# Scores of 64 new queries against 320 keys: from two full-precision matmuls with the queries as 64 weight columns each to four split-precision matmuls with the high and low queries side by side

## The chip, the cores and the metric

The kernel runs on one core of one Trainium2 chip. A core has TensorE (PE, matrix products, with weight loads shown as PEld), VectorE (DVE), ScalarE (ACT), GpSimd (POOL), and SyncE (SP), whose queue issues most DMA transfers. The engines run side by side; each takes its own instructions strictly in order and waits on semaphores for the others. The metric is the time of one execution on the device in microseconds (us), as the median of several executions; lower is better.

## What is computed

One layer of a streaming encoder for two groups that share all weights: the Prompt (256 positions) and the Sample (64 new positions behind 256 cached ones). The two are held together as 320 columns. The layer is a norm, a projection into q, k, v, two gating branches, stick-breaking attention, a spatial gate, a merge, an output projection, and a feed-forward block. The part that matters here is the attention, for each of 8 heads of width 128:

```python
z = einsum('bqhd,bkhd->bhqk', q, k) * 128 ** -0.5
mask = k_pos[None, :] < q_pos[:, None]
log_beta = log_sigmoid(z)
log_stay = where(mask, log_sigmoid(-z), 0.0)
log_rest = cumsum(log_stay, axis=3, reverse=True) - log_stay
w = where(mask, exp(log_beta + log_rest), 0.0)
o = einsum('bhqk,bkhd->bqhd', w, v)
```

For the Sample, q has 64 rows, and k has 320: 64 of its own and 256 from the cache. The mask cuts only inside the 64 own keys. All inputs and outputs are float32.

## The kernel before

Activations lie with the features on the 128 partitions and the 320 positions along the free axis. The large products keep float32 accuracy in a faster type: every operand is split into a high part (rounded to the type `float32r`, by ScalarE) and a low part (the rest, by VectorE), and three matmuls, high x high, high x low, low x high, add up in PSUM (`product`, lines 83 to 85). `weights` loads a half block of 128 x 1024 weights on SP's queue (line 70) and splits it: the copy to `wh` on ScalarE (line 75), the subtraction to `wl` on VectorE (line 76). Raw tiles have three buffers, split ones four, so loads and splits run some half blocks ahead of TensorE. A block of 16 row tiles is two half blocks of 24 matmuls.

`tick()` counts half blocks. `at(n, fn)` asks that `fn` is written into the program after half block n, so the attention's small steps are strewn between the matmuls of the projections. The program text is then turned into one order per engine by a scheduler that uses its own estimates of durations; instructions inside `keep_in_program_order` keep theirs.

The eight heads go in four pairs p. Pair 0 is projected in the opening phase. Each later pair takes twelve half blocks, k, q, v of one head and then of the other; `head_out` evicts each from PSUM, and GpSimd issues the stores of k and v (line 478). For a pair, `att_keys` loads the cached keys behind the new ones in the tile `k`; `att_parts` splits the Prompt's second query block and its keys with `parts`, which takes its tiles from the 32 slots of tag "B"; `att_scores` makes the scores. In `att_scores` the PSUM tiles `za` receive the Prompt's scores (one full float32 matmul for the diagonal block, line 387, and three split ones, line 389, for each head). The PSUM tile `zs` receives the Sample's: one full float32 matmul for each head (line 391), with the head's 64 queries as weights, so that head 0 writes rows 0 to 63 and head 1 rows 64 to 127. Lines 395 to 398 move the scores into two SBUF tiles z, adding a mask of large negative numbers where keys are hidden: `z[0]` gets the 256 past keys of the Sample, `z[1]` its 64 own ones.

What follows is a chain over these tiles: |z| (line 403), exp (404), ln (405) on ScalarE, then on VectorE line 406, backward running sums (413) and a subtraction (416), exp again on ScalarE (417 to 420), then the turning of the weights by DMA and the products with v (`att_out`). `attend` sets the half blocks at which these steps are written. There are eight PSUM banks: three tiles "acc" for the projections, four "aux", one "aux1".

Of the kernel before, what the change touches and what calls it, by code (L numbers as in the profile page):

```python
# [8 lines left out]
F32 = mybir.dt.float32  # L9
F32R = mybir.dt.float32r  # L10
AF = mybir.ActivationFunctionType
ALU = mybir.AluOpType

P = 128
TP = 256
TS = 64
T = TP + TS
# [7 lines left out]
PAST = 256  # L25
# [8 lines left out]
def stream_step(ctx: ExitStack, tc: tile.TileContext, xT, w_in, w_a, w_b, w_out, w_gu, w_down,  # L34
                gains, ws_t, bs, ck_t, cv, y_t, k_t, v_t, sv_t):
    nc = tc.nc
# [11 lines left out]
    def aux():  # L48
        return psum.tile([P, 512], F32, tag="aux", bufs=4, name="aux")
# [5 lines left out]
    state = {"tick": 0}  # L55
    later: dict[int, list] = {}

    def at(tick, fn, *a):
        assert tick > state["tick"], (tick, state["tick"])
        later.setdefault(tick, []).append((fn, a))  # L60
# [26 lines left out]
    def block(src, act):  # L87

        ps = acc()
        nk = len(act)  # L90
        for k0 in range(0, nk, HALF):
            n = min(HALF, nk - k0)
            w = weights(src[:, k0 * P : (k0 + n) * P], n)
            for j in range(n):
                product(ps, w, j, act[k0 + j], k0 + j == 0, k0 + j == nk - 1)
            tick()
        return ps[:, :T]

    def slot(tag):
        return big.tile([P, T], F32R, tag=tag, bufs=32, name=tag)  # L100

    def pair(name):
        return big.tile([P, 2 * T], F32, tag="D", bufs=8, name=name)
# [24 lines left out]
    def t320(tag, bufs=2, dt=F32):  # L128
        return tmp.tile([P, T], dt, tag=tag, bufs=bufs, name=tag)
# [92 lines left out]
    def use_w(b, wh, wl, c, n):  # L222

        for w, parts, last in ((wh, (0, 1), False), (wl, (0,), True)):
            for j in range(n):
                for h in range(2):
                    for i in parts:
                        nc.tensor.matmul(first[b][h][:, :T], w[:, (h * n + j) * P : (h * n + j + 1) * P],  # L228
                                         xs[c + j][i], start=not last and c + j + i == 0,
                                         stop=last and c + j == KD - 1)  # L230
# [61 lines left out]
    attn = {}  # L292
# [23 lines left out]
    Z, KT = 384, T + PAST  # L316
# [5 lines left out]
    mown = apool.tile([P, TS], F32, name="mown")  # L322
# [3 lines left out]
    ROWS = (slice(0, TS), slice(TS, P))  # L326
# [3 lines left out]
    def att_new(p):  # L330
        attn[p] = {"q": apool.tile([P, 2, T], F32, tag="q", bufs=2, name="q"),
                   "k": apool.tile([P, 2, KT], F32, tag="k", bufs=2, name="k"),
                   "v": apool.tile([P, 2, T], F32, tag="v", bufs=2, name="v")}
# [5 lines left out]
    def planes(name, n):  # L339
        return pair(name)[:, 0:n].bitcast(U16).rearrange("p (w n) -> p w n", w=2)  # L340

    def apart(to, src):
        nc.scalar.copy(out=to, in_=src.bitcast(U16).rearrange("p (n w) -> p w n", w=2))
# [18 lines left out]
        tc.keep_in_program_order(nc.sync.dma_start(out=cvt.rearrange("p i h d -> p i (h d)"),  # L362
                                                   in_=cv[:, :, 2 * p * P : (2 * p + 2) * P]))

    def parts(src):

        n = src.free_size()
        hi, lo = (slot("B")[:, 0:n] for _ in range(2))
        view = lambda t: t.rearrange("p (j d) -> p j d", j=src.shape[1]) if len(src.shape) == 3 else t
        nc.scalar.copy(out=view(hi), in_=src)  # L370
        nc.vector.tensor_tensor(out=view(lo), in0=src, in1=view(hi.bitcast(F32)), op=ALU.subtract)
        return hi, lo


# [2 lines left out]
    def att_parts(p):  # L377
        s = attn[p]
        s["qp"] = parts(s["q"][:, :, P:TP])
        s["kp"] = [parts(s["k"][:, j, 0:TP]) for j in range(2)]  # L380

    def att_scores(p):
        s = attn[p]
        q, k, qp = s["q"], s["k"], s["qp"]
        za, zs = (aux(), aux()), aux()
        for j in range(2):
            nc.tensor.matmul(za[j][:, 0:P], q[:, j, 0:P], k[:, j, 0:P], start=True, stop=True)  # L387
            for a, b in THREE:
                nc.tensor.matmul(za[j][:, P:Z], qp[a][:, j * P : (j + 1) * P], s["kp"][j][b], start=a + b == 0, stop=a == 1)  # L389
        for j, r in enumerate(ROWS):  # L390
            nc.tensor.matmul(zs[r, 0 : KT - TP], q[:, j, TP:T], k[:, j, TP:KT], start=True, stop=True)  # L391
        z = s["z"] = pair("z0"), pair("z1")[:, 0 : Z + TS]
        for j in range(2):
            diag = [t[:, 0:Z].rearrange("p (i t) -> p i t", i=3)[:, 0:3:2, :] for t in (z[j], za[j])]
            nc.vector.tensor_tensor(out=diag[0], in0=diag[1], in1=mdiag.unsqueeze(1).broadcast_to([P, 2, P]), op=ALU.add)
            nc.vector.tensor_copy(z[j][:, P : 2 * P], za[j][:, P : 2 * P])
        nc.vector.tensor_tensor(out=z[1][:, Z:], in0=zs[:, 0:TS], in1=mown, op=ALU.add)
        nc.vector.tensor_copy(z[0][:, Z:], zs[:, TS : TS + PAST])

        es = []  # L400
        for zz in z:
            e = pair("e")[:, : zz.shape[1]]
            nc.scalar.activation(out=e, in_=zz, func=AF.Abs)
            nc.scalar.activation(out=e, in_=e, func=AF.Exp, scale=-1.0)
            nc.scalar.activation(out=e, in_=e, func=AF.Ln, bias=1.0)
            nc.vector.scalar_tensor_tensor(out=e, in0=zz, scalar=0.0, in1=e, op0=ALU.max, op1=ALU.add)
            es.append(e)


        for j, lo, hi, begin in ((0, 0, P, 0.0), (0, P, Z, 0.0), (1, 0, P, 0.0), (1, P, Z, 0.0),  # L410
                                 (1, Z, Z + TS, 0.0), (0, Z, Z + PAST, es[1][:, Z : Z + 1])):
            back = es[j][:, lo:hi][:, ::-1]
            nc.vector.tensor_tensor_scan(out=back, data0=ones[:, 0:1].broadcast_to([P, hi - lo]), data1=back,
                                         initial=begin, op0=ALU.mult, op1=ALU.add)
        for zz, e in zip(z, es):
            nc.vector.tensor_tensor(out=zz, in0=zz, in1=e, op=ALU.subtract)
        nc.scalar.activation(out=z[0], in_=z[0], func=AF.Exp)
        nc.scalar.activation(out=z[1][:, 0:Z], in_=z[1][:, 0:Z], func=AF.Exp)
        for r in ROWS:
            nc.scalar.activation(out=wown[r, r], in_=z[1][r, Z:], func=AF.Exp)  # L420

        y = s["wp"] = planes("wp0", 5 * P), planes("wp1", 4 * P)
        apart(y[0], z[0])
        apart(y[1][:, :, 0:Z], z[1][:, 0:Z])
        apart(y[1][:, :, Z:], wown)
# [44 lines left out]
    def head_out(name, ps, h):  # L470
        s = attn[h // 2]
        o = s[name][:, h % 2, 0:T]
        if name == "q":
            nc.vector.scalar_tensor_tensor(out=o, in0=ps, scalar=QSCALE, in1=got["rx"],
                                           op0=ALU.mult, op1=ALU.mult)
        else:
            nc.vector.tensor_tensor(out=o, in0=ps, in1=got["rx"], op=ALU.mult)
            nc.gpsimd.dma_start(out=(k_t if name == "k" else v_t)[h], in_=o)
        if name == "v":
            j = h % 2  # L480
            if j == 0:
                s["vp"] = planes("vp", 5 * P)
            apart(s["vp"][:, :, j * TP : (j + 1) * TP], o[:, 0:TP])
            apart(s["vp"][:, :, 4 * P + j * TS : 4 * P + (j + 1) * TS], o[:, TP:T])
# [6 lines left out]
    def attend(p, now):  # L491
        at(now + 2, att_scores, p)
        at(now + 5, att_turn, p, "vt")
        at(now + 11, att_rows, p)
        at(now + 8, att_join, p, "vt")
        at(now + 12, att_turn, p, "wt")
        at(now + 14, att_join, p, "wt")
        at(now + 16, att_out, p)
# [2 lines left out]
    at(state["tick"] + 1, first_out)  # L501
    at(state["tick"] + 2, att_parts, 0)
    at(state["tick"] + 2, att_keys, 0)
    attend(0, state["tick"] + 2)
    at(state["tick"] + 14, gate_load)
    at(state["tick"] + 16, bias_load)
    for h in range(2, H):
        if h % 2 == 0:
            att_new(h // 2)
            at(state["tick"] + 11, att_keys, h // 2)  # L510
        for name, b in (("k", 1), ("q", 0), ("v", 2)):
            head_out(name, block(w_in[b * H + h], xs), h)
        if h % 2:
            att_parts(h // 2)
            attend(h // 2, state["tick"])
# [4 lines left out]
    for g in range(H):  # L520
        ps = block(w_in[4 * H + g], xs)
        t = t320("ev")
# [60 lines left out]
    for g in range(H):  # L583
        ps = block(w_in[3 * H + g], xs)
        t = t320("ev")
# [6 lines left out]
    for m in range(KD):  # L592
        gate = []
        for i in range(2):
            ps = block(w_in[5 * H + i * KD + m], xs)
            t = t320("ev")
# [8 lines left out]
        t = t320("mg", 1)  # L605
# [4 lines left out]
        hi = mpool.tile([P, T], F32R, tag="C", bufs=32, name="mh")  # L610
        lo = mpool.tile([P, T], F32R, tag="C", bufs=32, name="ml")
# [74 lines left out]
    ms, r = (const.tile([P, 3], F32, name=f"col{i}") for i in range(2))  # L686
# [68 lines left out]
```

## Time and profile before

| | |
|---|---|
| median of 3 runs | 1705.48 us |
| lowest, highest run | 1705.28 us, 2364.16 us |
| the profiled execution | 1705.09 us |
| its span, first to last instruction | 1703.3 us |
| granted TensorE clock, mean share | 0.998 |
| busy: TensorE, VectorE, ScalarE, GpSimd | 1692.7, 880.1, 677.2, 40.9 us |
| TensorE instructions | 11558 matmuls |

The time of an execution includes a little before and after the span. Busy times overlap between engines; what matters is which engine never rests and, for the others, when their results are due. A row of a list in order of time gives the start, the length, the engine and line, the operation, the tiles written and read, and in brackets how long the engine had been idle and what ended that. A group row gives the count, the busy time, the mean length of one in ns, and the idle time ahead of it. A page row with two numbers and a count in round brackets for each engine is a stretch of the run.

### The profile page before, as it was taken

Reading aid. Unit: us, or ns where it says so; the run is one execution under the profiler, and the core shown is the slowest. Engines: PE = TensorE matmul, PEld = TensorE weight load, DVE = VectorE, ACT = ScalarE, POOL = GpSimd, SP = SyncE. Lnnn points to the kernel's source line nnn. Section 1 sums busy time; section 2 is a strip of 40 time slices with the busy share of each in tenths; the row PEclk is TensorE's granted clock in tenths of the full one; section 3 lists DMA queues with packets and bytes.
Section 4 is the critical chain, followed back from the end, with each engine's and each line's share of the span. In section 5 each row is a group of like instructions: output and inputs, shape, how many; then the busy total and the mean of one; then the engine's idle time right before and its main releaser. Section 6 shows DMA issues by size and latency. Waiting matters only on the chain.

```text
span 1703.3 us, 27412 instructions
## 1 busy us (share of the span) xinstructions
PE 1692.7 (99%) x11558; PEld 1689.7 (99%) x11558; DVE 880.1 (52%) x1134; ACT 677.2 (40%) x862; POOL 40.9 (2%) x64
## 2 busy tenths in 40 slices
PE   9999999999999999999999999999999999999997
PEld 9999999999999999999999999999999999999997
DVE  7666557544444445555444444444444444444454
ACT  7665555433333333444333332333333333333342
POOL 0000011000000000110000000000000000000000
PEclk9999999999999999999999999999999999999999
DMA  7576566444444445554444455444444554444453
GB/s 254 168 224 186 166 171 174 148 149 150 150 150 153 151 157 165 172 164 149 149 150 150 150 152 152 151 150 149 149 149 150 150 149 153 149 153 149 127 152 118
DMA packets 100155, 268.30 MB, mean 158 GB/s; under 512 B 28960, under 2 KB 35104, under 8 KB 100032
## 3 DMA queue, kind: packets, MB, share of 16 engines
q1 hardware_dynamic: 98800, 263.49, 50.1%
q0 software_dynamic: 1088, 3.02, 0.5%
q8 instruction: 90, 1.47, 0.3%
q14 instruction: 33, 0.27, 0.0%
q10 hardware_dynamic: 144, 0.05, 0.0%
HBM read 256.03 MB, written 5.51 MB: 154 GB/s over the span
## 4 chain that ended last, share of the span: by engine, by line
issue 55%; PE 44%; DVE 0%; ACT 0%; POOL 0%; POOLq 0%; DVEq 0%
PE acc L83 13%; PE acc L85 13%; PE acc L84 13%; PE aux L228 2%; PE acc L228 1%; PE aux L450 1%; DVE h L694 0%; PE aux L199 0%; PE aux L563 0%; PE aux L389 0%; PE aux L391 0%; PE aux L387 0%; POOL sq_h L183 0%; PE aux L692 0%; POOLq L741 0%
## 5 line engine op out<-in xcount | busy, mean ns | idle before, releaser
L75 ACT CAST wh<-raw 128x1024 fp32r<-128x1024 f32 x468 | 484.5, 1036 | 941.7 <-PE acc L84 744.0
L76 DVE TENSOR_TENSOR wl<-raw,wh 128x1024 fp32r<-128x1024 f32 x468 | 563.8, 1206 | 464.8 <-ACT wh L75 462.8
L83 PE MATMUL acc<-A,wh 128*128 128x320 f32 x2464 | 762.4, 309 | 0.0
L85 PE MATMUL acc<-A,wl 128*128 128x320 f32 x2464 | 761.4, 309 | 0.0
L84 PE MATMUL acc<-A,wh 128*128 128x320 f32 x2464 | 761.3, 309 | 0.0
L83 PEld LDWEIGHTS acc<-A,wh 128*128 128x128 f32 x2464 | 462.6, 188 | 2.0 <-issue 2.0
L84 PEld LDWEIGHTS acc<-A,wh 128*128 128x128 f32 x2464 | 462.6, 188 | 0.0
L85 PEld LDWEIGHTS acc<-A,wl 128*128 128x128 f32 x2464 | 462.6, 188 | 0.0
L85 PE MATMUL acc<-B,wl 128*128 128x320 f32 x960 | 296.6, 309 | 0.0
L83 PE MATMUL acc<-B,wh 128*128 128x320 f32 x960 | 296.6, 309 | 0.0
L84 PE MATMUL acc<-B,wh 128*128 128x320 f32 x960 | 296.6, 309 | 0.0
L83 PEld LDWEIGHTS acc<-B,wh 128*128 128x128 f32 x960 | 180.2, 188 | 0.0
L84 PEld LDWEIGHTS acc<-B,wh 128*128 128x128 f32 x960 | 180.2, 188 | 0.0
L85 PEld LDWEIGHTS acc<-B,wl 128*128 128x128 f32 x960 | 180.2, 188 | 0.0
L83 PE MATMUL acc<-mh,wh 128*128 128x320 f32 x256 | 79.1, 309 | 0.0
L84 PE MATMUL acc<-ml,wh 128*128 128x320 f32 x256 | 79.1, 309 | 0.0
L85 PE MATMUL acc<-mh,wl 128*128 128x320 f32 x256 | 79.1, 309 | 0.0
L653 DVE TENSOR_TENSOR bb<-acc,rh 128x320 f32<-128x320 f32 x44 | 21.6, 491 | 56.5 <-PE acc L85 56.5
L650 DVE TENSOR_TENSOR ev<-acc,rh 128x320 f32<-128x320 f32 x44 | 21.6, 492 | 56.1 <-PE acc L85 56.1
L83 PEld LDWEIGHTS acc<-mh,wh 128*128 128x128 f32 x256 | 48.0, 188 | 0.0
L84 PEld LDWEIGHTS acc<-ml,wh 128*128 128x128 f32 x256 | 48.0, 188 | 0.0
L85 PEld LDWEIGHTS acc<-mh,wl 128*128 128x128 f32 x256 | 48.0, 188 | 0.0
(174 smaller groups left out, 717.2 us busy)
## 6 DMA issues: line engine op xcount, KB each, us to landing
raw<-w_gu SPq DMA_DIRECT2D x176, 512.0 KB, 3.6
raw<-w_in SPq DMA_DIRECT2D x141, 512.0 KB, 3.8
raw<-w_down SPq DMA_DIRECT2D x80, 512.0 KB, 3.6
raw<-w_out SPq DMA_DIRECT2D x32, 512.0 KB, 3.6
raw<-w_a SPq DMA_DIRECT2D x16, 512.0 KB, 3.5
raw<-w_b SPq DMA_DIRECT2D x16, 512.0 KB, 3.5
raw<-w_down SPq DMA_DIRECT2D x16, 256.0 KB, 2.7
x<-xT SPq DMA_DIRECT2D x8, 320.0 KB, 8.0
```

The source lines that it names most:

```text
L75: nc.scalar.copy(out=wh[:, : n * P], in_=raw[:, : n * P])
L76: nc.vector.tensor_tensor(out=wl[:, : n * P], in0=raw[:, : n * P], in1=wh[:, : n * P].bitcast(F32), op=ALU.subtract)
L83: nc.tensor.matmul(ps[:, :T], a, x[0], start=first, stop=False)
L84: nc.tensor.matmul(ps[:, :T], a, x[1], start=False, stop=False)
L85: nc.tensor.matmul(ps[:, :T], b, x[0], start=False, stop=last)
L228: nc.tensor.matmul(first[b][h][:, :T], w[:, (h * n + j) * P : (h * n + j + 1) * P], xs[c + j][i], start=not last and c + j + i == 0, stop= ...
L450: mm = lambda out, a, b, first, last: nc.tensor.matmul(out, a, b, start=first, stop=last, skip_group_check=True)
L650: nc.vector.tensor_tensor(out=t, in0=pg, in1=got["rh"], op=ALU.mult)
L653: nc.vector.tensor_tensor(out=u, in0=pu, in1=got["rh"], op=ALU.mult)
```

## The change

For the Sample, the queries of each head are split into a high and a low half, and both halves lie side by side as 128 weight columns (`qs`). The Sample's 320 keys are split too (`ks`, in the new step `att_past`), with the low half of the keys subtracted on GpSimd. For each head two split matmuls, high keys and low keys, go into a PSUM tile of its own: rows 0 to 63 hold the products of the high queries, rows 64 to 127 those of the low ones. ScalarE copies the rows that lie on the other head's side across into an SBUF tile `low`, VectorE adds the two halves into z in four adds, and GpSimd adds the mask to the 64 own keys. `att_scores` now takes four "aux" tiles instead of three. Pair 0's attention steps are written one half block later, and its `att_past` one half block before its scores; for the later pairs the cached keys are loaded after the sixth half block instead of the eleventh, and `att_past` follows after the ninth.

```diff
-    def parts(src):
+    def parts(src, engine=None):
...
-        nc.vector.tensor_tensor(out=view(lo), in0=src, in1=view(hi.bitcast(F32)), op=ALU.subtract)
+        (engine or nc.vector).tensor_tensor(out=view(lo), in0=src, in1=view(hi.bitcast(F32)), op=ALU.subtract)
...
+        own = s["qs"] = slot("B")[:, 0 : 4 * TS].rearrange("p (j w t) -> p j w t", j=2, w=2)
+        new = s["q"][:, :, TP:T]
+        nc.scalar.copy(out=own[:, :, 0], in_=new)
+        nc.vector.tensor_tensor(out=own[:, :, 1], in0=new, in1=own[:, :, 0].bitcast(F32), op=ALU.subtract)
+
+    def att_past(p):
+        s = attn[p]
+        s["ks"] = [parts(s["k"][:, j, TP:KT], nc.gpsimd) for j in range(2)]
...
-        za, zs = (aux(), aux()), aux()
+        za, zs = (aux(), aux()), (aux(), aux())
...
-        for j, r in enumerate(ROWS):
-            nc.tensor.matmul(zs[r, 0 : KT - TP], q[:, j, TP:T], k[:, j, TP:KT], start=True, stop=True)
+        for j in range(2):
+            for b in range(2):
+                nc.tensor.matmul(zs[j][:, 0 : KT - TP], s["qs"][:, j].rearrange("p w t -> p (w t)"), s["ks"][j][b],
+                                 start=b == 0, stop=b == 1)
...
-        nc.vector.tensor_tensor(out=z[1][:, Z:], in0=zs[:, 0:TS], in1=mown, op=ALU.add)
-        nc.vector.tensor_copy(z[0][:, Z:], zs[:, TS : TS + PAST])
+        low = t320("mg", 1)
+        for j, r in enumerate(ROWS):
+            nc.scalar.copy(out=low[r, :], in_=zs[j][ROWS[1 - j], 0:T])
+        for j, r in enumerate(ROWS):
+            nc.vector.tensor_tensor(out=z[0][r, Z:], in0=zs[j][r, TS : TS + PAST], in1=low[r, TS:], op=ALU.add)
+            nc.vector.tensor_tensor(out=z[1][r, Z:], in0=zs[j][r, 0:TS], in1=low[r, 0:TS], op=ALU.add)
+        nc.gpsimd.tensor_tensor(out=z[1][:, Z:], in0=z[1][:, Z:], in1=mown, op=ALU.add)
...
-    attend(0, state["tick"] + 2)
+    at(state["tick"] + 4, att_past, 0)
+    attend(0, state["tick"] + 3)
...
-            at(state["tick"] + 11, att_keys, h // 2)
+            at(state["tick"] + 6, att_keys, h // 2)
+            at(state["tick"] + 9, att_past, h // 2)
```

## The prediction, made before the changed kernel was run

> **What bounds the kernel now.** I read the page first: the share of each engine, then TensorE's own list of waits.
>
> ```profile
> span 1703.3 us, 27412 instructions
> PE 1692.7 (99%) x11558; PEld 1689.7 (99%) x11558; DVE 880.1 (52%) x1134; ACT 677.2 (40%) x862; POOL 40.9 (2%) x64
> PE aux L199 <- PEq L738: 0.8, 1, 0.8
> PE aux L692 <- POOL col L688: 0.2, 1, 0.2
> ```
>
> TensorE is busy for 1692.7 of 1703.3 us and in the whole run waits for data once, 0.2 us near the end. So a saving counts only if it shortens TensorE's stream, and a loss comes only if something makes TensorE wait. The edit therefore has two questions: how long the Sample's score matmuls hold TensorE, and how much spare time lies between each producer and the matmul that reads it.
>
> For the first, the chain of work around the scores of the second pair of heads. Its columns are start, length, what; because matmuls overlap, each piece runs from the end before it to its own end, so the pieces add up.
>
> ```profile
> 19.89 7.04 PE aux L228 x48
> 99.52 0.15 PE acc L85
> 100.47 0.36 PE aux L389 x3
> 100.83 0.69 PE aux L391 x4
> 101.52 0.35 PE acc L83
> 101.87 0.14 PE acc L84
> ```
>
> Undisturbed split matmuls with 320 columns come every 7.04 / 48 = 0.147 us. L391, the two full fp32 matmuls of the Sample's queries (two records each), takes 0.69 us, and the ordinary L83 behind it takes 0.35 instead of 0.147. The section costs 0.69 + 0.35 = 1.04 us a pair, four times in the run.
>
> **TensorE's part of the change.** Removed: L391's 0.69 us a pair. Added: four matmuls with 128 weight columns and 320 moving columns in the split type, exactly the shape of the main stream, so 4 x 0.147 = 0.59 us. They follow L389 and precede L83, both with 128 weight columns, so I also give L83 its ordinary 0.147 back. Saved: 1.04 - 0.59 - 0.147 = 0.305 us a pair, 1.22 us in all. Bounds from the nearest rows: at L389's 0.36 / 3 = 0.12 each, 0.41 a pair, 1.7 in all; at L391's own 0.69 / 4 each, with L83's excess staying, nothing is saved. I take 0.147, because the row has the same shape and type.
>
> The Trainium skill, TensorEngine Tiling (Array Packing), Key Properties, says that going from one tiling mode to another drains the array. By that rule both edges of the 64-column section are drains and go away with it: L83's excess of 0.2 us then goes, as the sum assumes.
>
> **What prepares the operands.** Per pair the edit adds on ScalarE the high half of the new queries, two copies of 320 keys and two copies of the partner's rows out of PSUM; on VectorE the low half of the queries and four adds in place of one add and one copy; on GpSimd two subtractions over 320 keys and the mask add. The nearest rows:
>
> ```profile
> L117 ACT CAST B<-bb 128x320 fp32r<-128x320 f32 x24 | 11.0, 459 | 9.9 <-DVE bb L573 7.8 <-DVE bb L654 0.6
> L117 ACT CAST B<-aux 128x320 fp32r<-128x320 f32 x3 | 1.3, 424 | 1.6 <-PE aux L450 1.6
> L343 ACT COPY vp<-v 128x128 uint16<-128x128 uint16 x8 | 2.4, 296 | 0.0
> L397 DVE TENSOR_TENSOR z<-aux,mown 128x64 f32<-128x64 f32 x4 | 0.9, 222 | 0.3
> L398 DVE COPY z<-aux 128x256 f32<-128x256 f32 x4 | 1.7, 414 | 0.0
> L183 POOL TENSOR_TENSOR sq_h<-sq_h,sq 128x320 f32<-128x320 f32 x14 | 15.3, 1095 | 473.7 <-ACT sq L182 473.7
> L328 POOL COPY mown<-mdiag 64x64 f32<-64x64 f32 x2 | 0.5, 242 | 0.0
> 48.00:84.00 36.00, 36.00 (x248) 35.37 (x247) 25.44 (x43) 22.86 (x34) 3.78 (x7) 1.00 0.55 168
> ```
>
> ScalarE: 0.30 + 2 x 0.46 + 2 x 0.42 = 2.1 us a pair. VectorE: about 0.28 for the queries, 2 x 0.41 + 2 x 0.22 for the adds, less 0.64 removed: 0.9 us. GpSimd: 2 x 1.10, and a mask add between 0.24 (a 64-column copy) and 1.10 (a 320-column add); I take 0.4, nearer the 64-column row. The last row is the stretch of the first pair: of 36 us VectorE (third pair of numbers) is busy 25.4 and ScalarE 22.9, so as load this fits four times over, and it costs nothing while the time of each piece is free. If that cover were gone, the whole of VectorE's and ScalarE's additions, 3 us a pair, would be the price.
>
> The cached keys are also loaded earlier. For pairs 1 to 3 the load moves from the eleventh to the sixth half block, past five weight loads in SP's queue. That queue mostly waits for buffers, so one issue of 0.4 us changes nothing:
>
> ```profile
> SPq L70 <- DVE wl L76: 1360.1, 454, 10.6
> 38.68 0.38 SPq L356 DMA_DIRECT2D k<-ck_t  x1
> DMA to landing us min/median/max: 3.9/4.4/5.9
> ```
>
> The parts of those keys are made five half blocks (5 x 24 x 0.147 = 17.6 us) before their use: free. Pair 0 has one half block, 3.52 us, and its scores move back by as much. Its keys are issued at 38.7 and land by 44.6.
>
> ```profile
> 62.36 1.05 ACT L75 CAST wh<-raw 128x1024 fp32r<-128x1024 f32 x1 [2.47 <-PE acc L84]
> 57.77 0.54 POOL L478 DMA_DIRECT2D k_t<-k  x1
> 63.52 0.76 PE L391 MATMUL aux<-k,q 128*64 128x320 f32 x4
> ```
>
> ScalarE idles 2.47 us until 62.36, so both key copies can be done by 60.9; GpSimd is free from 58.3 and ends its two subtractions by 63.1. They are needed at 63.52 + 3.52 = 67.0: 3.9 us spare, no cost. If ScalarE takes them only behind the weight cast (63.4), GpSimd ends near 66.6, still in time.
>
> **The wait that matters: the chain behind the scores.** From the scores on, ScalarE and VectorE alternate over z, and the weight splits for TensorE stand in the same in-order queues. In pair 0, by VectorE and ScalarE's lists in order of time:
>
> ```profile
> 64.39 0.22 DVE L397 TENSOR_TENSOR z<-aux,mown 128x64 f32<-128x64 f32 x1
> 64.54 0.41 DVE L398 COPY z<-aux 128x256 f32<-128x256 f32 x1
> 64.87 1.22 DVE L76 TENSOR_TENSOR wl<-raw,wh 128x1024 fp32r<-128x1024 f32 x1
> 64.98 1.21 ACT L403 ACTIVATE e<-z 128x640 f32<-128x640 f32 x2 [1.58 <-DVE z L398]
> 70.80 1.36 DVE L406 SCALAR_TENSOR_TENSOR e<-z,e 128x640 f32<-128x640 f32 x2 [4.72 <-ACT e L405]
> 76.36 1.22 DVE L76 TENSOR_TENSOR wl<-raw,wh 128x1024 fp32r<-128x1024 f32 x1
> 78.68 0.31 PE L85 MATMUL acc<-A,wl 128*128 128x320 f32 x1
> ```
>
> L406 blocks VectorE for 4.72 us, and the low weights of the ninth half block are queued behind L406 to L416: done at 77.58, read by L85 at 78.68. That 1.10 us is the smallest margin I found, pairing the casts and subtractions with the half blocks in order; the next is 1.47 us, in the chain of pair 3 (these weights end at 216.91, read at 218.38):
>
> ```profile
> 215.70 1.21 DVE L76 TENSOR_TENSOR wl<-raw,wh 128x1024 fp32r<-128x1024 f32 x1
> 218.38 0.31 PE L85 MATMUL acc<-A,wl 128*128 128x320 f32 x1
> ```
>
> Shifting pair 0 by one half block moves both chain and reader by 3.52 us, so the margin starts at 1.10 again. Now the edit's effect. ScalarE's two copies (0.42 each) run while VectorE still evicts the Prompt's scores. Four adds follow at steps of 0.33 (64.54 to 64.87) and 0.15 (64.39 to 64.54): z0 is whole after 0.33 + 0.15 + 0.41 = 0.89 us instead of 0.15 + 0.41 = 0.56, so the chain starts 0.33 later. z1 is whole after 1.03, plus two hand-overs of some 0.05 each, plus the mask's 0.4: 1.53 us. ScalarE reaches z1 only after |z0|, at 0.89 + 0.65 = 1.54, so the mask on GpSimd is just covered. TensorE finishes the Sample's scores 0.10 earlier and reads the next weights 0.31 earlier. Margin left: 1.10 - 0.33 + 0.10 - 0.31 = 0.56 us. It bears a further delay of 0.56 us, and pair 3's 0.93. If a mask of 1.10 us shows instead, 0.7 us are added and TensorE waits 0.14.
>
> **Sum.** Against the profiled execution (1705.09 us; its span 1703.3, 1.8 around it): 1705.09 - 1.22 = 1703.9, span 1702.1. The median of the runs shown, 1705.48, is 0.39 higher, so the forecast for the median is **1704.3 us**. About 2% (34 us) is what a measurement of this kernel tells from no change: the forecast is far inside that.
>
> **Rivals.** (A) **GpSimd and VectorE get in each other's way.** The rows where GpSimd runs beside VectorE today:
>
> ```profile
> 217.02 1.76 POOL L183 TENSOR_TENSOR sq_v<-sq_v,sq 128x320 f32<-128x320 f32 x1 [2.38 <-ACT sq L182]
> 217.97 1.10 DVE L371 TENSOR_TENSOR B<-av,B 128x256 fp32r<-128x256 f32 x1
> L371 DVE TENSOR_TENSOR B<-k,B 128x256 fp32r<-128x256 f32 x8 | 3.0, 418 | 0.0
> ```
>
> The GpSimd add, started while a weight subtraction (L76) was running, took 1.76 us instead of 1.10, and the VectorE subtraction started in its second half took 1.10 instead of 0.42. In pair 0 a weight subtraction stands right behind the last z add, so the mask would wait out its 1.22 us: z1 comes 1.1 us later, 0.54 us over the margin in pair 0, 0.2 in pair 3: 1704.3 + 0.7 = **1705.0**. Against it: ScalarE can do more of z0 first. The subtractions of the keys would cost VectorE 0.7 us each, but stand away from the two thin margins: nothing. The Trainium skill, SBUF — State Buffer, Who interferes with whom, calls this an exclusive lock between GpSimd reads and VectorE instructions with two SBUF inputs; the rows agree, and the rule speaks against this mask add.
>
> (B) **GpSimd's queue holds the mask back, and the run gets slower.** GpSimd also issues the stores of k and v, each after its eviction:
>
> ```profile
> 74.83 0.54 POOL L478 DMA_DIRECT2D v_t<-v  x1 [16.53 <-DVE v L477]
> ```
>
> Were the mask of pair 0 queued behind this store, it would wait for the v block, whose last matmul comes one half block (3.52 us) after the scores, then eviction 0.48 and store 0.54: about 3.2 us later than above. The margin of 0.56 gives out and TensorE waits 2.6: **1706.9**, slower than before. It decides from 0.56 us of delay in pair 0, and from 1.8 us the whole gain is lost. Against it: the mask is ready before the v block ends, and an order made by readiness puts it first.
>
> (C) **The gaps stay.** If L83's excess comes from the scores as a whole, not from the 64-column section, only 0.69 - 0.59 = 0.10 us a pair is saved: 1705.48 - 0.4 = **1705.1**. Against it: by the chain the excess stands behind L391 in the first and the last pair too, as in the second:
>
> ```profile
> 63.59 0.69 PE aux L391 x4
> 64.28 0.34 PE acc L83
> 194.66 0.34 PE acc L83
> ```
>
> **How the numbers follow.** Forecast 0.50, with its own range 1703.8 (the bound of 1.7 us saved) to 1704.6; A 0.22; B, or another delay of that chain beyond the margin, 0.14; C 0.11; 0.03 for an order of the queues that I don't foresee. Forecast, A and C lie between 1703.8 and 1705.2 and hold 0.83; unknown mask and lock costs reach into B, so I take 1703.8 to 1706.2. None of the named cases comes near 2%: within 0.97; slower 0.02 from the unforeseen orders; faster 0.01, since no row offers TensorE 34 us.
>
> **What would show it.** Right: in the chain the new score matmuls take about 0.59 us a pair with the following L83 at 0.15; TensorE's list of waits stays at 1.0 us; the span is near 1702.1; pair 0's scores stand near 65.8 us. A: the mask on GpSimd over 1 us long beside an L76, and |z1| late. B: the mask after a v store. C: L83 still at 0.35. I am wrong if TensorE waits for wl or for the key parts, or if the span is above 1703.3.

## The result and the profile after

The changed kernel takes 1713.38 us in the median (1712.89 to 1714.67, six executions), the kernel before 1705.22 (1705.02 to 1705.48, five executions). The ratio is 1.005, with a 95% interval of 1.0039 to 1.0061: 8.2 us slower, well inside 2%, but outside the predicted range of 1703.8 to 1706.2 and in the other direction. A sixth execution of the kernel before took 2364.16 us and stands in no comparison here, but it is one of the three behind the 1705.48 us that the prediction started from.

From the page of the changed kernel:

```profile
span 1712.7 us, 27477 instructions
PE 1695.1 (99%) x11558; PEld 1693.6 (99%) x11558; DVE 885.6 (52%) x1146; ACT 683.9 (40%) x882; POOL 54.3 (3%) x76
```

From its list of waits, the two of TensorE's weight loads that are new and long (engine and line, what it waited for, us in total, times, longest):

```profile
PEld aux L467 <- DVE wt L353: 6.5, 1, 6.5
PEld acc L85 <- DVE wl L76: 1.0, 1, 1.0
```

Line 467 is the matmul helper of `att_out` in the changed file (450 before), line 353 the copy that puts the turned attention weights together. TensorE now waits once for 6.5 us, in pair 0's `att_out`, and once for 1.0 us for low weights, near 227 us, behind the chain of pair 3. The rows around the long wait, from the chain that ended last (start, length, what; some ordinary matmuls are left out):

```profile
118.29 5.48 DMA turned<-wp
123.80 0.89 DVE wt L353
124.70 0.76 DVE wt L353
125.50 3.78 PE aux L467 x16
129.28 0.27 PE acc L85
129.55 0.27 PE acc L83
130.88 0.85 PE aux L467 x4
131.96 0.15 PE acc L83
```

The transfer that turns pair 0's attention weights is issued at 118.29 us, and TensorE, which takes its instructions in order, stands still until its result is copied. When it starts again, the ordinary matmuls come every 0.27 us instead of 0.147. The view by stretches shows the clock; the three numbers at the end of a row are the granted clock, the DMA share and GB/s:

```profile
118.00:126.00 8.00, 1.74 (x11) 1.48 (x10) 4.69 (x6) 5.56 (x10) 0.55 (x1) 0.72 1.00 207
126.00:132.00 6.00, 6.00 (x29) 6.00 (x28) 2.28 (x4) 1.24 (x5) 0.00 (x0) 0.52 1.06 229
132.00:140.00 8.00, 8.00 (x56) 8.00 (x55) 7.04 (x9) 3.38 (x6) 3.17 (x3) 1.00 0.52 187
```

`att_out` takes 3.78 + 0.85 us here and 2.28 in the kernel before (row below, from its chain, for pair 1); with the six ordinary matmuls between 129.28 and 130.88 us, 0.27 instead of 0.147 each, the slow stretch costs 3.1 us. The Trainium skill, TensorE: Matmul & The Clock Gate, Part 1, says that an idle window of about 3.4 us takes the clock to one half, and that a busy window of the same length gives it back. The half agrees: in shorter stretches the granted clock is 0.50 from 123 to 130 us. The length of the wait does not: 2.3 us were enough in e3 (last section).

```profile
155.32 2.28 PE aux L450 x20
```

The books close, to the rounding of these rows: 6.5 + 3.1 + 1.0 us lost and 1.2 us gained (0.31 us a pair, worked out under "Why the prediction was wrong") make 9.4 us, and the spans differ by 1712.7 - 1703.3 = 9.4.

**Why the turn is late.** SP's queue in order of time, first in the kernel before, then in the changed one:

```profile
79.12 2.22 SPq L348 DMA_TRANSPOSE turned<-vp  x1
82.79 5.15 SPq L348 DMA_TRANSPOSE turned<-wp  x2
```

```profile
85.59 1.74 SPq L348 DMA_TRANSPOSE turned<-vp  x1
100.20 18.04 SPq L70 DMA_DIRECT2D raw<-w_in  x5
118.29 4.29 SPq L348 DMA_TRANSPOSE turned<-wp  x2
```

The turn of wp moved by 35 us, ten times the 3.52 us of the shift, although the tiles it reads are ready at 86.8 us (ScalarE's last copy into them, line 343, ends there). In the built program, the tiles of tag "D" (`z0`, `z1`, `e`, `wp0`, `wp1`, `vp`, `turned`; eight slots) get their slots strictly in the order in which they are written in the program. Around the place in question (pair in brackets):

```
before: vp(1)  turned vt(0)  turned wt(0) x2   z0(1) z1(1) e(1) e(1) wp0(1) wp1(1)
after:  vp(1)  turned vt(0)  z0(1) z1(1) e(1) e(1) wp0(1) wp1(1)   turned wt(0) x2
```

`attend(0)` writes this turn twelve half blocks behind its base. With the base one later, it falls into the fifteenth half block, and pair 1's scores are written in the fourteenth. Pair 1's scores ask for six slots first, only five are free, and the two `turned` tiles queue behind them; the first takes over the slot of an `e` of pair 1, which is free only when pair 1's chain has used it (line 433, at 116.2 us). The last 2.1 us to 118.29 it stands in SP's queue behind a weight load, which waits for a buffer until 117.9. So the half block of shift made pair 0's last step wait for pair 1's whole chain.

### The profile page after: what moved, and what is told of

Its sections match the earlier page's. It is cut to its first block, busy times and chain, and to the rows that moved or that the text cites. A ratio compares the mean times of both kernels' runs of the same rounds, so it can differ in the third digit from the quotient of the medians.

```text
span 1712.7 us, 27477 instructions
## 1 busy us (share of the span) xinstructions
PE 1695.1 (99%) x11558; PEld 1693.6 (99%) x11558; DVE 885.6 (52%) x1146; ACT 683.9 (40%) x882; POOL 54.3 (3%) x76
## 4 chain that ended last, share of the span: by engine, by line
issue 55%; PE 41%; DVE 2%; DMA 1%; ACT 1%; POOL 0%; SPq 0%; POOLq 0%; DVEq 0%; ACTq 0%
PE acc L85 13%; PE acc L83 13%; PE acc L84 13%; PE aux L228 2%; PE acc L228 1%; PE aux L467 1%; DVE wl L76 0%; DVE h L713 0%; DMA turned<-wp 0%; DMA turned<-vp 0%; DMA raw<-w_in 0%; DVE e L430 0%; PE aux L582 0%; POOL z L415 0%; DVE e L423 0%
## 5 line engine op out<-in xcount | busy, mean ns | idle before, releaser
L83 PE MATMUL acc<-A,wh 128*128 128x320 f32 x2464 | 762.3, 309 | 0.0
L83 PEld LDWEIGHTS acc<-A,wh 128*128 128x128 f32 x2464 | 463.0, 188 | 0.0
L83 PE MATMUL acc<-B,wh 128*128 128x320 f32 x960 | 296.6, 309 | 0.0
L83 PEld LDWEIGHTS acc<-B,wh 128*128 128x128 f32 x960 | 180.2, 188 | 0.0
L83 PE MATMUL acc<-mh,wh 128*128 128x320 f32 x256 | 79.1, 309 | 0.0
L83 PEld LDWEIGHTS acc<-mh,wh 128*128 128x128 f32 x256 | 48.1, 188 | 0.0
```

The costliest lines, as they stand in the source:

```text
L83: nc.tensor.matmul(ps[:, :T], a, x[0], start=first, stop=False)
```

## Experiments

Times are medians. Each round ran on a chip of its own, and the kernel before, on the same chip, gave 1705.24, 1705.27 and 1705.20 us.

**First round: is it the place in the written order?**

e1 puts pair 0 back to its half blocks of before:

```diff
-    at(state["tick"] + 4, att_past, 0)
-    attend(0, state["tick"] + 3)
+    at(state["tick"] + 3, att_past, 0)
+    attend(0, state["tick"] + 2)
```

> The new scores stay, but pair 0's attention steps go back to the half blocks of before (scores after the fourth, key parts after the third). Theory S (slots in written order: the turn of pair 0's attention weights is written behind pair 1's scores, so its target tiles get their slots of tag D only when pair 1's chain gives some back): the turn of wt is issued near 83 us as before, TensorE's 6.3 us wait and the slow clock behind it are gone; 1705.25 - 1.2 + up to 1.0 of pair 3's wait for low weights = 1704.0 to 1705.1. Rival L (the longer chain with ScalarE's copies and GpSimd's mask makes the turned weights late): the wait of about 6 us stays, 1711 or more.

Measured: 1706.70 us (ratio 1.0008, interval 1.0000 to 1.0017). The wait on wt is gone, so L falls. The size was missed by 1.6 us: there are three waits for low weights, not one, behind the chains of pairs 0, 1 and 3 (list of waits of e1):

```profile
PE acc L85 <- DVE wl L76: 2.4, 3, 1.2
```

e2 takes the kernel before and makes only the shift:

```diff
-    attend(0, state["tick"] + 2)
+    attend(0, state["tick"] + 3)
```

> The kernel before with only pair 0's attention written one half block later; its scores are the old ones. Theory S: the turn of wt of pair 0 is issued behind pair 1's chain, near 115 to 118 us, TensorE waits about 6 us in pair 0's att_out and then runs some 6 us at about half clock: 1705.25 + 8 to 9.5 = 1713 to 1715. Rival L: nothing to wait for, 1705.3.

Measured: 1710.88 us (1.0030, 1.0020 to 1.0041). The old scores with the shift alone lose 5.6 us, less than the 8 to 9.5 expected: by the expected wait, though a shorter one, with a slow clock behind it (e2: SP's queue, then the list of waits):

```profile
115.15 4.44 SPq L348 DMA_TRANSPOSE turned<-wp  x2
```

```profile
PE aux L450 <- DVE wt L353: 2.7, 1, 2.7
```

The turn is issued at 115.15 instead of 118.29 us, since pair 1's old chain gives its slots back sooner. I had taken the 6 us over from the changed kernel without allowing for that.

e3 moves only that turn, ahead of pair 1's scores:

```diff
-        at(now + 12, att_turn, p, "wt")
+        at(now + 12 - (p == 0), att_turn, p, "wt")
```

> The changed kernel with one step moved: the turn of pair 0's attention weights is written one half block earlier, ahead of pair 1's scores. Theory S: turn issued near 87 us, no wait on wt: 1704.0 to 1705.1. Rival E (the turn is held by the order on SP's queue, behind a later weight load): the same. Rival L: 1711 or more.

e4 puts it into the same half block, behind pair 1's scores:

```diff
-        at(now + 12, att_turn, p, "wt")
+        if p:
+            at(now + 12, att_turn, p, "wt")
...
             attend(h // 2, state["tick"])
+            if h == 3:
+                at(state["tick"] + 2, att_turn, 0, "wt")
```

> As the run before it, in the same half block, but written behind pair 1's scores instead of ahead of them. Theory S: the tiles come late again, turn near 118 us, TensorE waits about 6 us: 1713 to 1714.5. Rival E: the place on SP's queue is that of the run before, so no wait: 1704.0 to 1705.1.

Measured: e3 1708.58 us (1.0019, 1.0010 to 1.0028), e4 1713.94 us (1.0051, 1.0038 to 1.0064). The two differ in nothing but which of two steps of one half block is written first. SP's queue and the list of waits of e3, then the list of waits of e4:

```profile
86.86 7.37 SPq L348 DMA_TRANSPOSE turned<-wp  x2
```

```profile
PE acc L85 <- DVE wl L76: 3.0, 2, 2.3
```

```profile
PE aux L467 <- DVE wt L353: 6.2, 1, 6.2
```

With the turn first (e3) it is issued at 86.86 us and nobody waits on wt; written second (e4), the wait is back at 6.2 us. That rules out the place in SP's queue (E) as the cause and leaves the slots. But e3 stays 3.5 us above the range expected, because of a wait of 2.3 us for low weights right behind pair 1's chain, followed by a slow clock. So a second loss, which e1 shows alone, comes from the chain behind the scores.

**Second round: the chain.** In e1, pair 0: instructions of ScalarE, GpSimd and VectorE, each engine's in order of time (start, length, engine, line; in brackets the idle time before it and what ended it):

```profile
65.29 0.74 ACT L420 ACTIVATE e<-z 128x640 f32<-128x640 f32 x1 [0.63 <-DVE z L413]
66.87 0.58 ACT L420 ACTIVATE e<-z 128x448 f32<-128x448 f32 x1 [0.84 <-POOL z L415]
65.48 1.36 POOL L415 TENSOR_TENSOR z<-z,mown 128x64 f32<-128x64 f32 x1 [1.99 <-DVE z L414]
65.43 1.23 DVE L76 TENSOR_TENSOR wl<-raw,wh 128x1024 fp32r<-128x1024 f32 x1
77.75 2.35 DVE L76 TENSOR_TENSOR wl<-raw,wh 128x1024 fp32r<-128x1024 f32 x2
```

The mask on GpSimd starts 0.05 us after a weight subtraction and ends 0.18 us after it; ScalarE idles 0.84 us for it; the subtractions behind the chain start at 77.75 us, 1.39 later than before (76.36). That is rival A at its place. Four kernels move the mask, all on e1.

e5, the mask on VectorE at the same place in the text:

```diff
-        nc.gpsimd.tensor_tensor(out=z[1][:, Z:], in0=z[1][:, Z:], in1=mown, op=ALU.add)
+        nc.vector.tensor_tensor(out=z[1][:, Z:], in0=z[1][:, Z:], in1=mown, op=ALU.add)
```

> Pair 0 early as in the run e1, and the mask is added by VectorE instead of GpSimd. Theory G (the mask on GpSimd takes 1.36 us beside a weight subtraction, ScalarE idles 0.84 us for it, and every subtraction behind the chain comes that much later): the chain is about 1 us shorter, TensorE's waits for low weights of pair 0 (0.8) and pair 3 (0.8) go, the third (1.3) shrinks or goes; 1704.2 to 1705.4. Rival W (the waits come from the added casts, copies and adds themselves): 1706 to 1707.5 as in e1.

e6, the low half of the keys on VectorE as well:

```diff
-        s["ks"] = [parts(s["k"][:, j, TP:KT], nc.gpsimd) for j in range(2)]
+        s["ks"] = [parts(s["k"][:, j, TP:KT]) for j in range(2)]
```

> As e5, and VectorE also makes the low half of the keys, so GpSimd has nothing of the change. Theory G with spare time on VectorE before the scores: as e5 within 0.5 us, since the key parts are made away from the chain (two subtractions of about 0.45 us a pair). Rival W: slower than e5 by 1 us or more, because VectorE has 0.9 us a pair more in front of the weight subtractions.

Measured: e5 1710.34 us (1.0026, 1.0016 to 1.0036), e6 1709.86 us (1.0023, 1.0013 to 1.0033). For e5 the expectation was wrong by 5 us; e6 stayed within the expected 0.5 us of e5. VectorE's and ScalarE's lists of e5 show what went wrong (line 421 is exp, 422 is ln):

```profile
66.51 1.23 DVE L76 TENSOR_TENSOR wl<-raw,wh 128x1024 fp32r<-128x1024 f32 x1
67.66 0.22 DVE L415 TENSOR_TENSOR z<-z,mown 128x64 f32<-128x64 f32 x1
70.94 0.74 ACT L422 ACTIVATE e<-e 128x640 f32<-128x640 f32 x1
71.70 1.28 ACT L421 ACT_TABLE_LOAD   x1
72.99 0.58 ACT L421 ACTIVATE e<-e 128x448 f32<-128x448 f32 x1
74.53 1.28 ACT L422 ACT_TABLE_LOAD   x1
```

The scheduler set the 0.22 us mask behind the weight subtraction, so z1 came later, and it set ln of z0 ahead of exp of z1. That the one led to the other is likely, since the order is the old one in e8, but not shown. In these rows ScalarE loads its function table anew each time it changes between the two, 1.28 us each: two more loads a pair (e5's groups; behind the bar us in total and mean ns of one):

```profile
L422 ACT ACT_TABLE_LOAD x8 | 10.3, 1283 | 0.1
L421 ACT ACT_TABLE_LOAD x5 | 6.4, 1283 | 0.1
```

The changed kernel has four and one of them. e6's low keys on VectorE change nothing beside that (0.5 us less, within the spread of both), so beside e5's longer chain it makes no difference which engine makes them.

e7 leaves the mask on GpSimd, but adds it to the copied rows, ahead of VectorE's adds; e8 does the same on VectorE:

```diff
             nc.scalar.copy(out=low[r, :], in_=zs[j][ROWS[1 - j], 0:T])
+        nc.gpsimd.tensor_tensor(out=low[:, 0:TS], in0=low[:, 0:TS], in1=mown, op=ALU.add)
...
-        nc.gpsimd.tensor_tensor(out=z[1][:, Z:], in0=z[1][:, Z:], in1=mown, op=ALU.add)
```

> As e1, with the mask on GpSimd but added to the copied rows (low), ahead of VectorE's adds instead of behind them. Theory G: GpSimd then runs beside VectorE's evictions out of PSUM and not beside a weight subtraction, so the mask takes 0.3 to 0.5 us and is covered; 1704.2 to 1705.4. If GpSimd is slow by itself (1.3 us whatever runs beside it), VectorE waits for it instead: 1706 to 1707.

> As e7 with VectorE adding the mask to the copied rows: one more 64-column add (0.2 us) in front of the four adds. Theory G: as e5, 1704.2 to 1705.4. Rival W: 1706 to 1707.5.

Measured: e7 1704.98 us (0.9998, 0.9989 to 1.0007), e8 1705.06 us (0.9998, 0.9989 to 1.0007). Both as expected. The group of the mask in the changed kernel, then in e7:

```profile
L415 POOL TENSOR_TENSOR z<-z,mown 128x64 f32<-128x64 f32 x4 | 5.3, 1330 | 17.4 <-DVE z L414 17.4
```

```profile
L412 POOL TENSOR_TENSOR mg<-mg,mown 128x64 f32<-128x64 f32 x4 | 1.3, 321 | 12.0 <-ACT mg L411 12.0
```

The same add of 128 x 64 takes 1.33 us beside a weight subtraction with two operands in SBUF and 0.32 us where VectorE reads PSUM. So GpSimd is not slow by itself; the place of the mask makes it slow. The Trainium skill, SBUF — State Buffer, Who interferes with whom, gives this as a lock between GpSimd's reads and VectorE instructions with two SBUF inputs, and the two rows agree.

**Third round: what is left.** In e7's trace TensorE waits for nothing new, yet its executions spread from 1703.77 (the one in the trace) to 1705.75. In that trace the low weights of one half block come 0.17 us before their use, queued on VectorE behind a copy that waits 4.80 us for a transfer (VectorE in order of time):

```profile
129.35 0.90 DVE L353 COPY wt<-turned 128x1280 uint16<-128x1280 uint16 x1 [4.80 <-DMA turned<-wp]
130.14 1.21 DVE L76 TENSOR_TENSOR wl<-raw,wh 128x1024 fp32r<-128x1024 f32 x1
```

e9 keeps that copy behind the subtractions written ahead of it:

```diff
-        nc.vector.tensor_copy(to.bitcast(U16).rearrange("p (n w) -> p w n", w=2), src)
+        return nc.vector.tensor_copy(to.bitcast(U16).rearrange("p (n w) -> p w n", w=2), src)
...
-            together(wt[:, 0 : 5 * P], t[0])
+            tc.keep_in_program_order(together(wt[:, 0 : 5 * P], t[0]))
```

> As e7 (pair 0 early, mask on the copied rows), and the first copy of the turned weights is kept behind the weight subtractions written ahead of it on VectorE, so that none of them queues behind a copy that waits for a transfer. If the thin margin there (0.17 us in e7's trace) is what cost e7 its gain in most executions: 1704.0 to 1704.7, the 1.2 us of the score matmuls in full or nearly. If not, 1705.0 as e7.

Measured: 1704.07 us, 1703.83 to 1704.32 in eleven executions, span 1702.1 us in the trace; the kernel before, on the same chip, never fell under 1704.89 in 28. The ratio is 0.9993 with an interval of 0.9984 to 1.0002, so the interval does not exclude no difference, while the two sets of times do not overlap. VectorE makes the low weights in question 3.3 us earlier than in e7 (130.14):

```profile
126.82 1.23 DVE L76 TENSOR_TENSOR wl<-raw,wh 128x1024 fp32r<-128x1024 f32 x1 [0.89 <-ACT wh L75]
```

The predicted saving of 1.2 us is there once nothing eats it.

The last three leave pair 0 late. e10 is e3 with e7's mask, e11 the changed kernel with e7's mask alone, e12 is e10 with e9's copy.

> The changed kernel with pair 0 late as it is, the turn of pair 0's weights ahead of pair 1's scores (as e3) and the mask on the copied rows (as e7). If the mask on GpSimd was behind e3's wait of 2.3 us for low weights: 1704.0 to 1705.5. If the shift itself crowds pair 1's half blocks: 1706.5 to 1708.5.

> The changed kernel with the mask moved to the copied rows alone; the turn stays behind pair 1's scores. Theory S and G: the wait for the turned weights stays and gets about 1 us shorter with pair 1's chain, pair 3's wait for low weights goes: 1710.5 to 1712.3. If the mask were the whole cause: 1705.

> As e10 with the copy of the turned weights kept behind the weight subtractions as in e9: 1704.0 to 1705.0 if the shift has no cost of its own, else as e10.

Measured: e10 1705.29 us (0.9998, 0.9990 to 1.0007), e11 1710.86 us (1.0033, 1.0021 to 1.0044), e12 1706.90 us (1.0013, 1.0004 to 1.0022). e10 and e11 came as expected. e10 is 3.3 us faster than e3, so the mask was behind most of e3's loss: the wait behind pair 1's chain fell from 2.3 to 1.2 us, and the slow clock behind it is gone. e11 takes 2.5 us off the changed kernel and keeps a wait of 4.3 us on wt. So of the 8.1 us between the changed kernel and e10 the mask's place makes 2.5 us, and the written order of the turn the other 5.6; mended in the other order (e3 first) they are 3.3 and 4.8. e12 missed: with the late pair 0 the kept copy does harm, and single executions reach 1710.12. Its trace does not show how: it is of one of the faster executions (1705.35 us), and the wait of 1.3 us behind pair 1's chain is e10's too (1.2). What crowds pair 1 there I did not separate. With both faults mended the shift costs nothing that stands out of the spread without the kept copy (e10 against e7, 0.3 us) and 2.8 us with it (e12 against e9).

## Why the prediction was wrong

**TensorE's part was right.** Pair 2 in the chain that ended last of the changed kernel:

```profile
156.08 0.36 PE aux L399 x3
156.45 0.58 PE aux L402 x4
157.03 0.15 PE acc L83
157.18 0.15 PE acc L84
```

The four matmuls take 0.58 us (0.59 predicted), and L83 behind them 0.15 instead of 0.35: rival C falls, and with it goes the excess that the 64-column section left behind. That the width made it and not the float32 type is not shown by a run of its own, but L389 stands behind L387, a float32 matmul with 128 weight columns, without an excess: 0.36 / 3 = 0.12 us for 256 columns, in proportion to 0.147 for 320. Saved 0.69 + 0.35 - 0.58 - 0.15 = 0.31 us a pair, 1.2 in all. The base of the sum, 1705.48, was 0.2 to 0.3 us high; 1705.2 - 1.2 = 1704.0 is what e9 came to (1704.07).

**The step that failed** is the sentence that shifting pair 0 "moves both chain and reader by 3.52 us, so the margin starts at 1.10 again". I followed the z chain and the key parts through the shift and left out the later steps that `attend` moves with them. The turn of the weights is one: it went past pair 1's scores in the written order, and both draw on the same eight slots. No wait, queue or busy share of the trace before shows that; it had to be read from the code, by listing every `at` of pair 0 against those of pair 1 (12 + 3 against 12 + 2) and the tiles each of them takes. Its price was 5.6 us by itself (e2) and 6.7 with the longer chain (the changed kernel against e1). The 0.03 for an unforeseen order was far too small for a change that moves seven steps of a written schedule.

**Rival A was right in mechanism and place, but I gave it 0.22.** The mask took 1.33 us where 0.4 was assumed, |z1| came 0.84 us late, and pair 3's margin broke, while pair 0's held in the changed kernel and broke only in e1. Pair 3's subtractions stand behind VectorE's copy of the turned v (changed kernel, VectorE in order of time):

```profile
224.94 0.91 DVE L353 COPY av<-turned 128x1280 uint16<-128x1280 uint16 x1 [2.65 <-DMA turned<-vp]
225.73 3.04 DVE L76 TENSOR_TENSOR wl<-raw,wh 128x1024 fp32r<-128x1024 f32 x2
```

That copy waits 2.65 us for its transfer, against 1.61 before, and the two subtractions take 3.04 us instead of 2.34, with another GpSimd add (line 183, 225.54 to 226.55) beside the first. The sum had neither: it counted the chain's delay straight into the margin. With the mask moved (e11) TensorE's wait there is gone. The cost of A was mis-sized: 0.7 us was named, while e11 against the changed kernel gives 2.5, because the chain also sets when slots come back (the wait on wt is 4.3 us there instead of 6.5), and e1 against e7 gives 1.7, with waits at three places where the sum had two. The rows quoted for A (1.76 instead of 1.10 us) already had this case in them, so 0.4 us was the wrong end to choose.

**Rival B** did not occur: the mask ran at 69.35 us, ahead of the v store at 72.27. Its mechanism, a late chain that starves the low weights, is what A did.

**Nothing on the key parts or the loads of the cached keys:** TensorE waited for neither.

## What to carry to other kernels

A step moved by one place in a written schedule must be checked against every step that it passes, for the buffers both take and not only for its data: here two tiles queued for slots behind a chain that started 16 us after their own data were ready. Where a chain ends in queues that feed the bound engine, keep its links in one order and out of each other's way: a 64-column add cost 1.0 us more beside a two-operand subtraction, and one placed a little later went with two more table loads a pair. When a small gain vanishes, look for margins of tenths of a microsecond; e9 needed three repairs for 1.2 us.

## What I had not expected of the hardware

A short wait costs more than its length. In e3, TensorE waited 2.3 us for low weights; the stretches of the wait and behind it:

```profile
115.00:117.60 2.60, 0.34 (x3) 0.07 (x1) 2.60 (x6) 1.75 (x2) 0.00 (x0) 1.00 0.00 0
117.60:121.00 3.40, 3.33 (x12) 3.33 (x13) 3.37 (x6) 2.11 (x5) 0.00 (x0) 0.51 0.55 153
```

The clock then stood at 0.51 for 3.4 us. In e10, where TensorE waited 1.2 us at the same place, it stayed at 1.00:

```profile
116.00:118.00 2.00, 0.93 (x6) 0.93 (x7) 2.00 (x3) 0.17 (x1) 0.00 (x0) 1.00 0.00 0
118.00:120.00 2.00, 2.00 (x16) 2.00 (x15) 1.97 (x4) 1.70 (x5) 0.00 (x0) 1.00 0.82 252
```

The traces of e2 and e6, each with a wait of 2.7 us, show the stretch behind it like this, and those of e1 and e12, with waits of 1.2 and 1.3 us, stay at 1.00:

```profile
122.40:127.00 4.60, 4.56 (x24) 4.56 (x25) 2.34 (x4) 1.61 (x4) 0.00 (x0) 0.63 1.09 212
134.60:139.00 4.40, 4.36 (x19) 4.36 (x20) 4.40 (x8) 1.97 (x3) 0.54 (x1) 0.61 0.55 178
```

Taking the slow clock as 0.5, as it stood from 123 to 130 us in the changed kernel, (1 - 0.63) x 4.6 / 0.5 and (1 - 0.61) x 4.4 / 0.5 are both 3.4 us at half clock, as in e3. By the rows of the result the changed kernel had (1 - 0.72) x 8 / 0.5 + (1 - 0.52) x 6 / 0.5 = 10.2 us, three times that, the first part of it within the wait. So in these traces the price of a wait steps up somewhere between 1.3 and 2.3 us, by 3.4 us at half clock, which is 1.7 us of TensorE's time. Whether it also matters when the wait falls is not shown.
